# Loading the last expert's first weights earlier and its second weights in four quarters, in a one-core mixture-of-experts layer

## The chip, the cores and the metric

The kernel runs on one core of one Trainium2 chip. The metric is device time in microseconds. TensorE is called PE here, its weight loads PEld, VectorE DVE, ScalarE ACT, GpSimd POOL, and SyncE SP. All weights come from HBM by DMAs that SP issues.

## What is computed

```python
def clamped_swiglu(h):
    gate = jnp.minimum(h[..., :D_EXPERT], SWIGLU_LIMIT)
    up = jnp.clip(h[..., D_EXPERT:], -SWIGLU_LIMIT, SWIGLU_LIMIT)
    return gate * jax.nn.sigmoid(SWIGLU_ALPHA * gate) * (up + 1.0)
...
mix = pool_mixer(h, pool_w[j], pool_scale[j])
h = layer_norm(DEEPNORM_ALPHA * h + mix, ln_g[i, 0], ln_b[i, 0])
ffn = moe(h, router_w[i], router_b[i], w1[i], b1[i], w2[i], b2[i])
h = layer_norm(DEEPNORM_ALPHA * h + ffn, ln_g[i, 1], ln_b[i, 1])
...
# in moe, for the rows of an expert e, top 4 of 32 experts for each token:
h = x_ext[tok] @ w1[e] + b1[e]
return (clamped_swiglu(h) @ w2[e] + b2[e]) * g[:, None]
```

There are 256 tokens after 16 meta tokens, 1024 channels, 32 experts, all in float32. For each expert `w1` is 1024 x 2048 (8 MB) and `w2` is 1024 x 1024 (4 MB). So about 400 MB of weights are read, each once.

## The kernel before

After a prologue (pooling mixer, first layer norm, router, places of the tokens in the experts' slots), a loop in Python goes over the 32 experts. Each expert has 64 slots; two experts make a pair. For expert `e` the loop

- issues the loads of `w1[e]` (four tiles of 2 MB) and then of `w2[e-1]` (two tiles of 2 MB);
- multiplies the gathered tokens `xg` with `w1[e]` (`mlp_in`, line 436);
- finishes the expert before it (`finish(e - 1)`): `mlp_out`, line 486, multiplies the activations `act` with `w2[e-1]` into the bank `ps_y`, and `out_evac`, lines 475 and 477, takes the result to `y` on ACT and DVE, scaled by the gate;
- computes `act` of expert `e` (`swiglu`: copies, transposes on PE in line 448, and elementwise work);
- on even `e`, adds the pair before it to `acc` (`combine`): four matmuls of line 506 with the pair's slot rows `s`, and four adds on DVE in line 508.

All weight tiles come from one pool of 8 buffers (`wpool`), in the order of the load calls. A tile is loaded when the matmuls on the tile eight places ahead of it have ended. All loads stand in SP's one queue, in that order.

After the loop the last expert's `w2` is loaded in two halves of the output columns (`load_w2_halves`, eight DMAs of 512 KB). Four banks `z` take `acc` through an identity matmul (line 615). Then for each half: `mlp_out_half` (line 495), the evacuation to `y`, the slot matmuls of line 621 that add `y` to `z`, and the `bn_stats` of line 108 over 512 columns. At the end `store` does the second layer norm from `z` on DVE and writes the output. A branch for experts with more than 64 tokens follows; it is not taken here.

The engines' order is that of the built program: each engine runs its own list strictly in order. A scheduler places the work of neighbouring calls; it put the identity matmuls of line 615 into the first-weight matmuls of the last expert, and between its transposes.

In the profile each fp32 matmul of the program shows as two rows with a weight load each, so that one weight tile of 2 MB is 16 matmul rows.

Of the kernel before, what the change touches and what calls it, by code (L numbers as in the profile page):

```python
# [9 lines left out]
F32 = mybir.dt.float32  # L10
# [27 lines left out]


@with_exitstack  # L40
def moe_trunk(ctx: ExitStack, tc: tile.TileContext, x, pool_w, aux_in, b1_in, w1, w2, b2, out):
    nc = tc.nc

    const = ctx.enter_context(tc.tile_pool(name="const", bufs=1))
    small = ctx.enter_context(tc.tile_pool(name="small", bufs=2))
    mid = ctx.enter_context(tc.tile_pool(name="mid", bufs=2))
    wpool = ctx.enter_context(tc.tile_pool(name="wpool", bufs=W_BUFS))
# [8 lines left out]
    def bank_t():  # L56
        return bank("t", 2)
# [38 lines left out]
    def spread(row, i, p):  # L96

        for k in range(4):
            spread.last = nc.tensor.matmul(p[:, k * P:(k + 1) * P], rhs=ident, start=True, stop=True,
                                           lhsT=row[:, 4 * i + k:4 * i + k + 1].to_broadcast([P, P]))  # L100
        return p

    def columns():
# [3 lines left out]
    def stats(st, z, i):  # L107
        nc.vector.bn_stats(st[:, i, :], z[i])
# [39 lines left out]
    with tc.tile_pool(name="pro", bufs=1) as pro:  # L148
# [94 lines left out]
        def turn(i):  # L243
            for t in range(NT):
                for k in range(4):
                    nc.tensor.transpose(zs[i][t][:, k * P:(k + 1) * P], zT[:, 4 * i + k, t * P:(t + 1) * P], ident)
                nc.vector.bn_stats(sts[t][:, i, :], zs[i][t])

        turn(1)
# [67 lines left out]
        for k0 in range(0, KC, 2):  # L317
            p = bank_t() if k0 < 4 else bank_o()
            for k in range(2):
                kk = k0 + k  # L320
                for t in range(NT):
                    gl = nc.tensor.matmul(p[:, k * P:(k + 1) * P], lhsT=h[:, t, kk * P:(kk + 1) * P],
                                          rhs=df[:, t, :2 * CAP], start=(t == 0), stop=(t == NT - 1))
# [48 lines left out]
    def load_w2(src):  # L372
        v = src.rearrange("(i p j) f -> i p j f", p=P, j=4)
        ts = []
        for i in range(KC // 4):
            wt = wpool.tile([P, 4, D], F32, tag="w", name="w2t")
            nc.sync.dma_start(out=wt, in_=v[i])
            ts.append(wt)
        return lambda k: ts[k // 4][:, k % 4, :].rearrange("p (c o s) -> p o c s", c=2, o=2)

    def load_w2_halves(src):

        v = src.rearrange("(i p j) f -> i p j f", p=P, j=4)
        ts = []
        for c in range(2):
            wt = wpool.tile([P, KC, 512], F32, tag="w", name="w2h")
            for k in range(0, KC, 2):
                i, j = divmod(k, 4)
                nc.sync.dma_start(out=wt[:, k:k + 2, :], in_=v[i, :, j:j + 2, c * 512:(c + 1) * 512])
            ts.append(wt)  # L390
# [7 lines left out]
    def gather(d):  # L398

        xg = columns()  # L400
        for k0 in range(0, KC, 4):
            p = bank_o() if k0 else bank_m()
            for k in range(4):
                cs = slice((k0 + k) * P, (k0 + k + 1) * P)
                for t in range(NT):
                    nc.tensor.matmul(p[:, k * P:(k + 1) * P], lhsT=h[:, t, cs], rhs=d[:, t, :2 * CAP],  # L406
                                     start=(t == 0), stop=(t == NT - 1))
            nc.scalar.copy(xg[k0 // 4].rearrange("p k s -> p (k s)"), p)  # L408
        return xg
# [31 lines left out]
    def swiglu(ph, bias):  # L441
        pre = []
        for u in range(2):
            hs = work.tile([P, 512], F32, tag="hs", name="hs", bufs=3)
            nc.scalar.copy(hs, ph[u])  # L445
            pt = bank_t()
            for j in range(4):
                nc.tensor.transpose(pt[:, j * P:(j + 1) * P], hs[:, j * P:(j + 1) * P], ident)  # L448
            a = work.tile([P, KC, CAP], F32, tag=f"a{u}", name=f"a{u}", bufs=1)
            nc.vector.tensor_add(a, pt.rearrange("p (c s) -> p c s", s=CAP),  # L450
                                 bias[:, :, u].unsqueeze(2).to_broadcast([P, KC, CAP]))
            pre.append(a)
        gate, up = pre
        nc.vector.tensor_scalar_min(gate, gate, LIMIT)  # L454
        sig = work.tile([P, KC, CAP], F32, tag="sig", name="sig", bufs=1)
        nc.scalar.activation(sig, gate, AF.Sigmoid, scale=SWIGLU_ALPHA)  # L456
        nc.vector.tensor_scalar(up, up, LIMIT, -LIMIT, op0=ALU.min, op1=ALU.max)
        nc.vector.tensor_mul(gate, gate, sig)  # L458
        act = work.tile([P, KC, CAP], F32, tag="act", name="act", bufs=2)
        nc.vector.scalar_tensor_tensor(act.rearrange("p c s -> p (c s)"), up.rearrange("p c s -> p (c s)"), 1.0,  # L460
                                       gate.rearrange("p c s -> p (c s)"), op0=ALU.add, op1=ALU.mult)
        return act


    def rows_of(o, i):

        r = (o ^ i) * CAP
        return slice(r, r + CAP)
# [18 lines left out]
                                 start=(n == 0), stop=(n == KC - 1))  # L487
        out_evac(py, y, slice(0, 512), sg, i)

    def mlp_out_half(act, wt, y, sg, i, c):  # L490
        py = [bank_t()[rows_of(o, i), :256] for o in range(2)]
        for n in range(KC):
            hf, j = divmod(n, 4)
            for o in range(2):
                nc.tensor.matmul(py[o], lhsT=act[:, 2 * j + hf, :], rhs=wt[:, n, o * 256:(o + 1) * 256],  # L495
                                 start=(n == 0), stop=(n == KC - 1))
        out_evac(py, y, slice(c * 256, (c + 1) * 256), sg, i)

    def outputs():
        return work.tile([P, 2, 512], F32, tag="y", name="y", bufs=2)  # L500
# [1 line left out]
    def combine(y, s):  # L502
        for t in range(NT):
            for o in range(2):
                p = bank_o()
                nc.tensor.matmul(p, lhsT=s[:, o, t * P:(t + 1) * P], rhs=y[:, o, :], start=True, stop=True)  # L506
                a = acc[:, t, :].rearrange("p (c o s) -> p o c s", c=2, o=2)[:, o]
                nc.vector.tensor_add(a, a, p.rearrange("p (c s) -> p c s", c=2))  # L508

    def add_bias():  # L510

# [69 lines left out]

    pairs[0] = df, xg0
    first = None
    for e in range(E):
        pair, i = divmod(e, 2)
        w1k = load_w1(w1[e])
        if e:
            w2s[e - 1] = load_w2(w2[e - 1])
        if i == 0:
            xg = pairs[pair][1]  # L590
        ph = mlp_in(lambda k: xg[k // 4][:, k % 4, i * CAP:(i + 1) * CAP], w1k)
        if e == 0:
# [76 lines left out]
```

## Time and profile before

| | |
|---|---|
| time, median of 3 runs | 983.04 us (982.01 to 983.7) |
| time of the profiled execution | 984.9 us |
| span of its instructions | 983.1 us |
| PE busy | 918.0 us, 93% |
| DVE, ACT busy | 228.7 us, 123.0 us |
| DMA, mean over the span | 414 GB/s, 407.13 MB |

The span runs from the first instruction of the program to the end of the last one; the time has what lies around it too, 1.8 us here. A share of busy time is an average over stages with different limits, so the end of the program has to be read by itself, in order of time.

### The profile page before, as it was taken

The numbers are of one execution on the slowest core, as the hardware profiler recorded it, in microseconds if no ns is written. First come the engines' busy times: TensorE is split into PE (matmuls) and PEld (weight loads), VectorE is DVE, ScalarE is ACT, GpSimd is POOL, SyncE is SP. The second block draws the span as 40 slices with busy tenths as digits, with TensorE's granted clock in tenths as the row PEclk, the third lists the DMA queues.
The fourth block names the chain that finished last, engine by engine and source line by source line (L and its number), as shares of the span: only waits on it lengthen the run. The fifth ranks groups of instructions, "written<-read, shape, count | busy, mean of one in ns | idle before, by whom it ended". The sixth has DMA issues, their size and how long they took to land.

```text
span 983.1 us, 10139 instructions
## 1 busy us (share of the span) xinstructions
PE 918.0 (93%) x4401; PEld 372.5 (38%) x4401; DVE 228.7 (23%) x470; ACT 123.0 (13%) x209; POOL 1.1 (0%) x9
## 2 busy tenths in 40 slices
PE   9999999999999999999989999799998989899894
PEld 6445343433334343433424333242433424233233
DVE  7242212112221212212211121211112211121214
ACT  1311111011111111011101111111011101011111
POOL 0000000000000000000000000000000000000000
PEclk9989999999999999999999999999999999999998
DMA  9999999999999999999999999999999999999992
GB/s 363 429 427 428 397 365 424 427 428 427 427 429 428 427 428 428 428 427 427 427 428 426 429 426 427 429 428 427 427 428 428 428 427 426 429 429 428 427 399 80
DMA packets 31072, 407.13 MB, mean 414 GB/s; under 512 B 3344, under 2 KB 3472, under 8 KB 6704
## 3 DMA queue, kind: packets, MB, share of 16 engines
q1 hardware_dynamic: 30976, 406.31, 97.9%
q8 instruction: 36, 0.59, 0.2%
q10 hardware_dynamic: 48, 0.13, 0.0%
q14 instruction: 12, 0.10, 0.0%
HBM read 405.38 MB, written 1.05 MB: 413 GB/s over the span
## 4 chain that ended last, share of the span: by engine, by line
PE 67%; DMA 28%; DVE 2%; ACT 1%; issue 1%; DVEq 0%; ACTq 0%
PE ps_h L436 33%; DMA w2t<-in_w 25%; PE ps_y L486 13%; PE ps_o L506 6%; DMA w1t<-in_w 3%; PE ps_o L406 3%; PE ps_m L406 3%; DVE y L477 1%; PE ps_m L425 1%; PE ps_t L448 1%; PE ps_m L419 1%; PE ps_t L173 1%; PE ps_t L495 1%; ACT hs L445 1%; PE ps_o L521 0%
## 5 line engine op out<-in xcount | busy, mean ns | idle before, releaser
L436 PE MATMUL ps_h<-w1t,xg 128*64 128x512 f32 x2048 | 464.0, 601 | 15.6 <-DMA w1t<-in_w 14.9
L436 PEld LDWEIGHTS ps_h<-w1t,xg 128*64 128x64 f32 x2048 | 141.0, 138 | 300.2 <-issue 260.0
L486 PE MATMUL ps_y<-w2t,act 128*64 128x512 f32 x992 | 222.7, 596 | 10.8 <-DMA w2t<-in_w 10.8
L450 DVE TENSOR_TENSOR a<-ps_t,b 128x512 f32<-128x512 f32 x64 | 44.2, 692 | 386.0 <-PE ps_t L448 382.4
L486 PEld LDWEIGHTS ps_y<-w2t,act 128*64 128x64 f32 x992 | 68.1, 137 | 142.3 <-issue 121.7
L445 ACT COPY hs<-ps_h 128x512 f32<-128x512 f32 x64 | 37.5, 585 | 330.5 <-PE ps_h L436 330.5
L506 PE MATMUL ps_o<-y,srow 128*128 128x512 f32 x120 | 58.4, 618 | 12.9 <-DVE y L477 12.9
L477 DVE TENSOR_SCALAR y<-ps_y,sgate 64x512 f32<-64x512 f32 x31 | 23.2, 750 | 130.5 <-PE ps_y L486 130.5
L508 DVE TENSOR_TENSOR acc<-acc,ps_o 128x512 f32<-128x512 f32 x60 | 41.3, 688 | 28.8 <-PE ps_o L506 28.8
L448 PE MATMUL ps_t<-ident,hs 128*128 128x128 f32 x256 | 42.4, 290 | 4.5 <-ACT hs L445 4.5
L475 ACT ACTIVATE y<-ps_y,sgate 64x512 f32<-64x512 f32 x31 | 21.1, 682 | 194.5 <-DVE y L477 194.5
L448 PEld LDWEIGHTS ps_t<-ident,hs 128*128 128x128 f32 x256 | 27.6, 143 | 38.7 <-ACT hs L445 36.1
L506 PEld LDWEIGHTS ps_o<-y,srow 128*128 128x128 f32 x120 | 19.0, 188 | 53.1 <-DVE y L477 26.1
L427 DVE COPY sgate<-ps_m 128x4 f32<-128x4 f32 x16 | 2.6, 162 | 155.9 <-PE ps_m L425 155.9
L406 PEld LDWEIGHTS ps_o<-disp,h 128*128 128x128 f32 x240 | 29.0, 191 | 22.7 <-issue 22.7
L406 PE MATMUL ps_m<-disp,h 128*128 128x128 f32 x240 | 31.7, 285 | 4.5 <-DVE sgate L427 4.5
L406 PE MATMUL ps_o<-disp,h 128*128 128x128 f32 x240 | 34.4, 287 | 0.0
L406 PEld LDWEIGHTS ps_m<-disp,h 128*128 128x128 f32 x240 | 28.4, 193 | 7.3 <-DVE sgate L427 5.7
L456 ACT ACTIVATE sig<-a 128x512 f32<-128x512 f32 x32 | 20.1, 630 | 68.2 <-DVE a L454 68.2
L458 DVE TENSOR_TENSOR a<-a,sig 128x512 f32<-128x512 f32 x32 | 22.1, 692 | 13.0 <-ACT sig L456 13.0
L408 ACT COPY xg<-ps_o 128x512 f32<-128x512 f32 x15 | 8.8, 585 | 123.1 <-PE ps_o L406 123.1
L460 DVE SCALAR_TENSOR_TENSOR act<-a,a 128x512 f32<-128x512 f32 x32 | 22.1, 691 | 1.1
(151 smaller groups left out, 268.8 us busy)
## 6 DMA issues: line engine op xcount, KB each, us to landing
w1t<-in_w SPq DMA_DIRECT2D x128, 2048.0 KB, 31.3
w2t<-in_w SPq DMA_DIRECT2D x62, 2048.0 KB, 29.4
w2h<-in_w SPq DMA_DIRECT2D x8, 512.0 KB, 22.7
xT<-in_x SPq DMA_DIRECT2D x2, 544.0 KB, 6.0
pw<-in_pool_w SPq DMA_DIRECT2D x2, 512.0 KB, 8.1
out<-xg SPq DMA_DIRECT2D x4, 256.0 KB, 2.9
b<-in_b SPq DMA_DIRECT2D x1, 256.0 KB, 9.1
aux<-in_aux SPq DMA_DIRECT2D x1, 164.0 KB, 3.1
```

Source lines behind the costliest of these rows:

```text
L406: nc.tensor.matmul(p[:, k * P:(k + 1) * P], lhsT=h[:, t, cs], rhs=d[:, t, :2 * CAP], start=(t == 0), stop=(t == NT - 1))
L436: last[0] = nc.tensor.matmul(ph[u][hf * CAP:(hf + 1) * CAP], lhsT=xcols(k), rhs=wk[:, u * D + hf * 512:u * D + (hf + 1) * 512], start=(k = ...
L445: nc.scalar.copy(hs, ph[u])
L448: nc.tensor.transpose(pt[:, j * P:(j + 1) * P], hs[:, j * P:(j + 1) * P], ident)
L450: nc.vector.tensor_add(a, pt.rearrange("p (c s) -> p c s", s=CAP), bias[:, :, u].unsqueeze(2).to_broadcast([P, KC, CAP]))
L458: nc.vector.tensor_mul(gate, gate, sig)
L460: nc.vector.scalar_tensor_tensor(act.rearrange("p c s -> p (c s)"), up.rearrange("p c s -> p (c s)"), 1.0, gate.rearrange("p c s -> p (c s ...
L475: nc.scalar.activation(y[r, o, cols], py[o], AF.Copy, scale=sg[r, o, i:i + 1])
L477: nc.vector.tensor_scalar_mul(y[r, o, cols], py[o], sg[r, o, i:i + 1])
L486: nc.tensor.matmul(py[o], lhsT=act[:, 2 * j + hf, :], rhs=wk[:, o], start=(n == 0), stop=(n == KC - 1))
L506: nc.tensor.matmul(p, lhsT=s[:, o, t * P:(t + 1) * P], rhs=y[:, o, :], start=True, stop=True)
L508: nc.vector.tensor_add(a, a, p.rearrange("p (c s) -> p c s", c=2))
```

## The change

Three things are edited. (1) The loads of `w1[31]` are called right after those of `w1[30]`, ahead of `w2[29]` and `w2[30]`; `mlp_in` and `swiglu` of expert 31 follow at once, and `finish(29)`, the `combine` of pair 14 and `finish(30)` come behind the loop. `act` gets a third buffer. (2) The last expert's `w2` is loaded and used in four quarters of the outputs, from an input of its own (`w2_last`) in which a quarter's 8 KB lie together for each partition; two quarters share one buffer. Each quarter has its own evacuation, slot matmuls and `bn_stats`. (3) The 128-channel blocks of a row stand in the order `PERM` in `acc`, `h`, the gains and the output, so that one quarter gives neighbouring columns in `z`; the host lays out `w2`, `b2` and the output to match.

```diff
+PERM = (0, 2, 1, 3, 4, 6, 5, 7)
...
-        return lambda k: ts[k // 4][:, k % 4, :].rearrange("p (c o s) -> p o c s", c=2, o=2)
+        return lambda k: ts[k // 4][:, k % 4, :].rearrange("p (o f) -> p o f", o=2)
...
+    def load_w2_quarters():
+
         ts = []
+        for q in range(4):
+            if q % 2 == 0:
+                wt = wpool.tile([P, 2, KC, 2, P], F32, tag="w", name="w2q")
+            for k, n in ((0, KC),) if q < 3 else ((0, 4), (4, 2), (6, 2)):
+                nc.sync.dma_start(out=wt[:, q % 2, k:k + n], in_=w2_last[q, :, k:k + n])
+            ts.append(wt[:, q % 2])
         return ts
...
-        act = work.tile([P, KC, CAP], F32, tag="act", name="act", bufs=2)
+        act = work.tile([P, KC, CAP], F32, tag="act", name="act", bufs=3)
...
+    def mlp_out_quarter(act, wq, y, sg, i, q):
+        py = [bank_t()[rows_of(o, i), :P] for o in range(2)]
         for n in range(KC):
             hf, j = divmod(n, 4)
             for o in range(2):
+                nc.tensor.matmul(py[o], lhsT=act[:, 2 * j + hf, :], rhs=wq[:, n, o],
                                  start=(n == 0), stop=(n == KC - 1))
+        out_evac(py, y, slice(q * P, (q + 1) * P), sg, i)
...
+        if e < E - 1:
+            w1s[e] = load_w1(w1[e])
+
+        if e == E - 2:
+            w1s[e + 1] = load_w1(w1[e + 1])
         if e:
             w2s[e - 1] = load_w2(w2[e - 1])
+        w1k = w1s[e]
...
-        else:
+        elif e < E - 2:
             finish(e - 1)
...
-        if e >= 2 and i == 0:
+        if 2 <= e < E - 2 and i == 0:
             s, _, y = pairs[pair - 1]
             combine(y, s)
-    wts = load_w2_halves(w2[E - 1])
+    wts = load_w2_quarters()
+    finish(E - 3)
+    s, _, y = pairs[E // 2 - 2]
+    combine(y, s)
+    finish(E - 2)
...
+    for q in range(4):
+        c, r = divmod(q, 2)
+        mlp_out_quarter(acts[E - 1], wts[q], y, sg, 1, q)
         for t in range(NT):
             for o in range(2):
+                nc.tensor.matmul(z[t][c][:, (2 * r + o) * P:(2 * r + o + 1) * P], lhsT=s[:, o, t * P:(t + 1) * P],
+                                 rhs=y[:, o, q * P:(q + 1) * P], start=False, stop=(o == 1),
+                                 skip_group_check=True)
+            nc.vector.bn_stats(sts[t][:, q, :], z[t][c][:, 2 * r * P:(2 * r + 2) * P])
```

The rows below are the built programs' own order, without times; a number after x counts the program's instructions (two profile rows for each matmul). The line numbers of the changed program are its own.

SP's queue at its end, before: the rows are the loads of `w1[30]`, `w2[29]`, `w1[31]`, `w2[30]` and the halves of `w2[31]`.

```order
L368 DMA w1t<-in_w 128x4096 x4
L377 DMA w2t<-in_w 128x4096 x2
L368 DMA w1t<-in_w 128x4096 x4
L377 DMA w2t<-in_w 128x4096 x2
L389 DMA w2h<-in_w 128x2x512 x8
```

SP's queue at its end, changed: the row x8 is `w1[30]` and `w1[31]`, the row x4 is `w2[29]` and `w2[30]`; a row of `w2[28]` stands ahead.

```order
L380 DMA w2t<-in_w 128x4096 x2
L371 DMA w1t<-in_w 128x4096 x8
L380 DMA w2t<-in_w 128x4096 x4
L391 DMA w2q<-in_w_last 128x2048 x3
L391 DMA w2q<-in_w_last 128x1024
L391 DMA w2q<-in_w_last 128x512 x2
```

The two tiles of `w2[29]` and the four of `w1[31]` changed places; `w2[30]` and `w2[31]` stand where they stood, the latter in six transfers and not eight.

PE from the transposes of expert 30 on, before (`xg_3865` and `xg_3866` are the tokens of pair 15; the first row of line 486 is `w2[29]`, the last `w2[30]`):

```order
L448 MATMUL ps_t<-ident,hs 128x128 x8
L486 MATMUL ps_y<-w2t,act 64x512 x16
L506 MATMUL ps_o<-y,srow 128x512 x4
L436 MATMUL ps_h<-w1t,xg_3865 64x512 x8
L615 MATMUL ps_o<-acc,ident 128x512 x2
L436 MATMUL ps_h<-w1t,xg_3865 64x512 x8
L436 MATMUL ps_h<-w1t,xg_3866 64x512 x16
L448 MATMUL ps_t<-ident,hs 128x128 x4
L615 MATMUL ps_h<-acc,ident 128x512
L448 MATMUL ps_t<-ident,hs 128x128 x4
L615 MATMUL ps_h<-acc,ident 128x512
L486 MATMUL ps_y<-w2t,act 64x512 x16
```

The same stretch of PE, changed (lines 438, 450, 488, 508 and 628 are the old 436, 448, 486, 506 and 615):

```order
L450 MATMUL ps_t<-ident,hs 128x128 x8
L438 MATMUL ps_h<-w1t,xg_3865 64x512 x16
L438 MATMUL ps_h<-w1t,xg_3866 64x512 x16
L450 MATMUL ps_t<-ident,hs 128x128 x8
L488 MATMUL ps_y<-w2t,act 64x512 x16
L508 MATMUL ps_o<-y,srow 128x512 x4
L488 MATMUL ps_y<-w2t,act 64x512 x8
L628 MATMUL ps_h<-acc,ident 128x512 x2
L488 MATMUL ps_y<-w2t,act 64x512 x8
L628 MATMUL ps_o<-acc,ident 128x512 x2
```

The `combine` of pair 14 (506, now 508) moved from ahead of the matmuls on `w1[31]` to behind them, and the four identity matmuls (615, now 628) from among these to the middle and the end of `w2[30]`.

PE behind that, before: the end of `w2[30]`, then the first half of `w2[31]` and the start of the second.

```order
L486 MATMUL ps_y<-w2t,act 64x512 x16
L495 MATMUL ps_t<-w2h,act 64x256 x16
L621 MATMUL ps_h<-y,srow 128x256 x2
L621 MATMUL ps_o<-y,srow 128x256 x2
L495 MATMUL ps_t<-w2h,act 64x256 x16
```

The same place, changed (497 and 636 are the old 495 and 621); the three rows from 497 on come four times in all.

```order
L628 MATMUL ps_o<-acc,ident 128x512 x2
L497 MATMUL ps_t<-w2q,act 64x128 x16
L636 MATMUL ps_h<-y,srow 128x128 x2
L636 MATMUL ps_o<-y,srow 128x128 x2
L497 MATMUL ps_t<-w2q,act 64x128 x16
```

Where two turns of matmuls, evacuation and slot matmuls stood, there are four, each with as many instructions of half the width.

## Rows read from the trace of the kernel before

**Rows 1.** The page: span, and GB/s in 40 equal slices of it.

```profile
span 983.1 us, 10139 instructions
...
GB/s 363 429 427 428 397 365 424 427 428 427 427 429 428 427 428 428 428 427 427 427 428 426 429 426 427 429 428 427 427 428 428 428 427 426 429 429 428 427 399 80
```

**Rows 2.** Busy time by stretch; PEclk is the granted clock's share of full speed.

```profile
core 0: us, PE busy (x) PEld busy (x) DVE busy (x) ACT busy (x) POOL busy (x), PEclk, DMA share, GB/s
900.00:944.00 44.00, 38.18 (x160) 12.19 (x158) 7.69 (x12) 3.16 (x5) 0.00 (x0) 1.00 1.01 428
...
958.00:966.00 8.00, 7.41 (x54) 4.44 (x52) 2.49 (x4) 1.15 (x2) 0.00 (x0) 1.00 0.35 132
966.00:976.00 10.00, 5.01 (x36) 3.16 (x32) 5.77 (x16) 2.89 (x6) 0.00 (x0) 0.90 0.01 3
```

**Rows 3.** The chain that ended last, in order of time: start us, us, what.

```profile
892.47 32.74 DMA w2t<-in_w
...
925.26 3.68 PE ps_y L486 x16
```

**Rows 4.** PE's timeline from 905 to 963: start, us, line, operation, [idle before <-releaser].

```profile
905.68 3.65 PE L436 MATMUL ps_h<-w1t,xg 128*64 128x512 f32 x16 [1.13 <-DMA w1t<-in_w]
...
915.47 3.65 PE L436 MATMUL ps_h<-w1t,xg 128*64 128x512 f32 x16 [1.23 <-DMA w1t<-in_w]
...
920.46 3.65 PE L486 MATMUL ps_y<-w2t,act 128*64 128x512 f32 x16
925.26 3.65 PE L486 MATMUL ps_y<-w2t,act 128*64 128x512 f32 x16 [1.15 <-DMA w2t<-in_w]
929.77 3.89 PE L506 MATMUL ps_o<-y,srow 128*128 128x512 f32 x8 [0.86 <-DVE y L477]
933.59 3.65 PE L436 MATMUL ps_h<-w1t,xg 128*64 128x512 f32 x16
937.18 1.98 PE L615 MATMUL ps_o<-acc,ident 128*128 128x512 f32 x4
939.09 10.52 PE L436 MATMUL ps_h<-w1t,xg 128*64 128x512 f32 x48
...
952.29 7.09 PE L486 MATMUL ps_y<-w2t,act 128*64 128x512 f32 x32
959.20 3.62 PE L495 MATMUL ps_t<-w2h,act 128*64 128x256 f32 x32
```

**Rows 5.** All engines' timeline from 959 to the end of PE's work.

```profile
959.21 3.17 PEld L495 LDWEIGHTS ps_t<-w2h,act 128*64 128x64 f32 x30 [0.28 <-issue]
959.42 0.74 DVE L477 TENSOR_SCALAR y<-ps_y,sgate 64x512 f32<-64x512 f32 x1 [5.53 <-PE ps_y L486]
...
962.87 0.49 DVE L477 TENSOR_SCALAR y<-ps_t,sgate 64x256 f32<-64x256 f32 x1 [2.70 <-PE ps_t L495]
...
963.41 1.13 PE L621 MATMUL ps_h<-y,srow 128*128 128x256 f32 x4 [0.59 <-DVE y L477]
...
965.34 3.67 PE L495 MATMUL ps_t<-w2h,act 128*64 128x256 f32 x32
...
970.56 1.03 PE L621 MATMUL ps_o<-y,srow 128*128 128x256 f32 x4
...
971.62 0.70 DVE L108 BATCH_NORM_STATS2 ln_st<-ps_o 128x6 f32<-128x512 f32 x1
```

**Rows 6.** SP's queue from 914 on: when the last weight loads were issued.

```profile
914.28 5.22 SPq L377 DMA_DIRECT2D w2t<-in_w  x2
924.15 31.14 SPq L389 DMA_DIRECT2D w2h<-in_w  x8
```

**Rows 7.** Groups by line and shape: busy us, mean ns of one, idle before.

```profile
L506 PE MATMUL ps_o<-y,srow 128*128 128x512 f32 x120 | 58.4, 618 | 12.9 <-DVE y L477 12.9
...
L406 PE MATMUL ps_o<-disp,h 128*128 128x128 f32 x240 | 34.4, 287 | 0.0
...
L425 PE MATMUL ps_m<-gates,disp 128*128 128x2 f32 x120 | 14.4, 242 | 0.7 <-ACT srow L421 0.7
```

More of the change, by code (lines that the diff above doesn't have):

```diff
@@ L40, in moe_trunk @@
 @with_exitstack
-def moe_trunk(ctx: ExitStack, tc: tile.TileContext, x, pool_w, aux_in, b1_in, w1, w2, b2, out):
+def moe_trunk(ctx: ExitStack, tc: tile.TileContext, x, pool_w, aux_in, b1_in, w1, w2, w2_last, b2, out):
     nc = tc.nc
@@ L99, in spread @@
             spread.last = nc.tensor.matmul(p[:, k * P:(k + 1) * P], rhs=ident, start=True, stop=True,
-                                           lhsT=row[:, 4 * i + k:4 * i + k + 1].to_broadcast([P, P]))
+                                           lhsT=row[:, PERM[4 * i + k]:PERM[4 * i + k] + 1].to_broadcast([P, P]))
         return p
@@ L245, in turn @@
                 for k in range(4):
-                    nc.tensor.transpose(zs[i][t][:, k * P:(k + 1) * P], zT[:, 4 * i + k, t * P:(t + 1) * P], ident)
+                    nc.tensor.transpose(zs[i][t][:, k * P:(k + 1) * P], zT[:, PERM[4 * i + k], t * P:(t + 1) * P],
+                                        ident)
                 nc.vector.bn_stats(sts[t][:, i, :], zs[i][t])
@@ L321, in moe_trunk @@
                 for t in range(NT):
-                    gl = nc.tensor.matmul(p[:, k * P:(k + 1) * P], lhsT=h[:, t, kk * P:(kk + 1) * P],
+                    gl = nc.tensor.matmul(p[:, k * P:(k + 1) * P], lhsT=h[:, t, PERM[kk] * P:(PERM[kk] + 1) * P],
                                           rhs=df[:, t, :2 * CAP], start=(t == 0), stop=(t == NT - 1))
@@ L378, in load_w2 @@
             ts.append(wt)
-        return lambda k: ts[k // 4][:, k % 4, :].rearrange("p (c o s) -> p o c s", c=2, o=2)
-    def load_w2_halves(src):
-        v = src.rearrange("(i p j) f -> i p j f", p=P, j=4)
+        return lambda k: ts[k // 4][:, k % 4, :].rearrange("p (o f) -> p o f", o=2)
+    def load_w2_quarters():
         ts = []
[L385 to L390, printed above, removed]
+        for q in range(4):
[4 more added lines that the diff above has]
+            ts.append(wt[:, q % 2])
         return ts
@@ L403, in gather @@
             for k in range(4):
-                cs = slice((k0 + k) * P, (k0 + k + 1) * P)
+                cs = slice(PERM[k0 + k] * P, (PERM[k0 + k] + 1) * P)
                 for t in range(NT):
@@ L488, in mlp_out @@
         out_evac(py, y, slice(0, 512), sg, i)
-    def mlp_out_half(act, wt, y, sg, i, c):
-        py = [bank_t()[rows_of(o, i), :256] for o in range(2)]
+    def mlp_out_quarter(act, wq, y, sg, i, q):
+        py = [bank_t()[rows_of(o, i), :P] for o in range(2)]
         for n in range(KC):
@@ L494, in mlp_out_half @@
             for o in range(2):
-                nc.tensor.matmul(py[o], lhsT=act[:, 2 * j + hf, :], rhs=wt[:, n, o * 256:(o + 1) * 256],
+                nc.tensor.matmul(py[o], lhsT=act[:, 2 * j + hf, :], rhs=wq[:, n, o],
                                  start=(n == 0), stop=(n == KC - 1))
-        out_evac(py, y, slice(c * 256, (c + 1) * 256), sg, i)
+        out_evac(py, y, slice(q * P, (q + 1) * P), sg, i)
     def outputs():
@@ L506, in combine @@
                 nc.tensor.matmul(p, lhsT=s[:, o, t * P:(t + 1) * P], rhs=y[:, o, :], start=True, stop=True)
-                a = acc[:, t, :].rearrange("p (c o s) -> p o c s", c=2, o=2)[:, o]
-                nc.vector.tensor_add(a, a, p.rearrange("p (c s) -> p c s", c=2))
+                a = acc[:, t, :].rearrange("p (q o s) -> p o q s", q=4, o=2)[:, o]
+                nc.vector.tensor_add(a, a, p.rearrange("p (q s) -> p q s", q=4))
     def add_bias():
@@ L583, in moe_trunk @@
     first = None
+    w1s = {}
     for e in range(E):
         pair, i = divmod(e, 2)
-        w1k = load_w1(w1[e])
+        if e < E - 1:
+            w1s[e] = load_w1(w1[e])
+        if e == E - 2:
+            w1s[e + 1] = load_w1(w1[e + 1])
         if e:
             w2s[e - 1] = load_w2(w2[e - 1])
+        w1k = w1s[e]
         if i == 0:
@@ L604, in moe_trunk @@
             prepare(pair + 1)
-        if e >= 2 and i == 0:
+        if 2 <= e < E - 2 and i == 0:
             s, _, y = pairs[pair - 1]
             combine(y, s)
-    wts = load_w2_halves(w2[E - 1])
+    wts = load_w2_quarters()
[3 more added lines that the diff above has]
+    finish(E - 2)
     z = [[bank_h() for _ in range(2)], [bank_o() for _ in range(2)]]
-    sts = [small.tile([P, 2, 6], F32, name="ln_st") for _ in range(NT)]
+    sts = [small.tile([P, 4, 6], F32, name="ln_st") for _ in range(NT)]
     for t in range(NT):
         for c in range(2):
-            nc.tensor.matmul(z[t][c], lhsT=ident, rhs=acc[:, t, c * 512:(c + 1) * 512], start=True, stop=False)
+            nc.tensor.matmul(z[t][c], lhsT=ident, rhs=acc[:, t, c * 512:(c + 1) * 512], start=True, stop=False,
+                             skip_group_check=True)
     s, sg, y = pairs[E // 2 - 1]
-    for c in range(2):
-        mlp_out_half(acts[E - 1], wts[c], y, sg, 1, c)
+    for q in range(4):
+        c, r = divmod(q, 2)
+        mlp_out_quarter(acts[E - 1], wts[q], y, sg, 1, q)
         for t in range(NT):
             for o in range(2):
-                nc.tensor.matmul(z[t][c][:, o * 256:(o + 1) * 256], lhsT=s[:, o, t * P:(t + 1) * P],
-                                 rhs=y[:, o, c * 256:(c + 1) * 256], start=False, stop=(o == 1))
-            stats(sts[t], z[t], c)
+                nc.tensor.matmul(z[t][c][:, (2 * r + o) * P:(2 * r + o + 1) * P], lhsT=s[:, o, t * P:(t + 1) * P],
+                                 rhs=y[:, o, q * P:(q + 1) * P], start=False, stop=(o == 1),
+                                 skip_group_check=True)
+            nc.vector.bn_stats(sts[t][:, q, :], z[t][c][:, 2 * r * P:(2 * r + 2) * P])
     store(z, g1_b, b1_b, sts)
@@ L640, with turned @@
     f = {n: np.asarray(a) for n, a in inputs.items()}
+    def turned(a):
+        return a.reshape(-1, KC, P)[:, list(PERM)].reshape(a.shape)
     pw = f["pool_w"].reshape(G, 2, P, GD).transpose(2, 0, 1, 3).reshape(P, -1)
@@ L654 @@
         "w1": f["w1"].reshape(E, KC // 2, 2, P, 2 * D).transpose(0, 1, 3, 2, 4).reshape(E, D, 2 * D),
-        "w2": f["w2"].reshape(E, KC // 4, 4, P, D).transpose(0, 1, 3, 2, 4).reshape(E, D, D),
-        "b2": f["b2"].reshape(E, D),
+        "w2": f["w2"].reshape(E, KC // 4, 4, P, 2, 2, 2, P).transpose(0, 1, 3, 2, 5, 4, 6, 7).reshape(E, D, D),
+        "w2_last": f["w2"].reshape(E, KC, P, 2, 2, 2, P)[-1].transpose(2, 4, 1, 0, 3, 5).reshape(4, P, KC, 2, P),
+        "b2": turned(f["b2"].reshape(E, D)),
     }
@@ L667 @@
     r = run_bass_kernel_spmd(nc, [arrays], core_ids=[0])
-    return r.results[0]["out"].reshape(1, SEQ, D)
+    return turned(r.results[0]["out"]).reshape(1, SEQ, D)
```

## The prediction

> **What bounds the kernel now.** I read the page first. The transfers run at about 428 GB/s in nearly every slice until the last two, and the last slice has 80 [rows 1]. So the body of the program is paced by the weights, and only its end can be moved by an order of loads. The stretches of the end say the same with a border: from 900 to 944 us the DMA share is 1.01 and PE is busy 38.18 of 44.00 us; from 958 on the share falls to 0.35 and then 0.01, while PE is busy 7.41 of 8.00 us [rows 2]. Somewhere between, the pace passes from DMA to PE. The chain of work that ended last names the place: its last DMA piece is the wait for a tile of `w2`, which ends at 925.26 [rows 3]; everything behind it is work of PE, and later of DVE.
>
> PE's timeline shows both regimes. Up to 925.26, a tile is 3.65 us of matmuls, and then PE waits for the next: starts at 905.68, 915.47 and 925.26 are two tiles apart each, so a tile arrives every 4.90 us [rows 4]. Behind 925.26 no row waits for a DMA. PE does the rest of `w2[29]`, the `combine` (929.77), `w1[31]` with the identity matmuls, `w2[30]` (952.29), and at 959.20 begins the last expert's second weights [rows 4]. At 925.26 eight tiles' worth of weights are still to come, 39 us at the cadence, so until about 964.4; PE's work takes 46 us, so the transfers end first, but not by much. Last come two turns of matmuls, evacuation and slot matmuls, up to 970.56 + 1.03 = 971.59, and 11.5 us of layer norm and output up to 983.1 [rows 1, 5].
>
> **The order of the loads.** It adds no bytes. The tiles have equal size and each still waits for the tile eight places ahead, whose release does not move: SP began the loads of `w2[31]` at 924.15 [rows 6], when PE had left the tile of 920.46 [rows 4], and a tile of `w1[31]` in that place is 16 rows of PE too. So I keep the arrivals and rename them. With 925.26 for the second tile of `w1[31]`: third 930.15, fourth 935.05, `w2[29]` 939.95 and 944.84, `w2[30]` 949.74 and 954.63, the quarters each 2.45 us later, 957.08 to 964.42. Now PE's list:
>
> - The fourth tile of `w1[31]` starts at 935.05. As with `w1[30]` (915.47 to 920.46, 4.99 us with the transposes [rows 4]) `w2[29]` starts at 940.04 and has done its first tile at 943.69. It waits until 944.84.
> - From there to the end of `combine` it takes as long as before: 933.59 - 925.26 = 8.33 us [rows 4], so 953.17.
> - `w2[30]` is two halves of (959.20 - 952.29) / 2 = 3.46 us, each followed by two identity matmuls of 939.09 - 937.18 = 1.91 us [rows 4]: 956.63, 958.54, 961.99, 963.90.
>
> The last expert's second weights start at 963.90 where they started at 959.20: **+4.7 us**. The reason in words: before, PE filled the gaps that the weights left with nothing but waits up to 925.26; now it waits up to 944.84, because a tile of `w1[31]` taken at its arrival costs 4.90 us and from the buffers it cost 3.65. The `combine` and the four identity matmuls, which ran while tiles arrived, now run behind nearly the last one. The activation of expert 31 is ready some 20 us earlier, but it never was late: `w2[30]` covered it.
>
> **The quarters.** Before, a turn was 3.62 us of matmuls, 0.59 of evacuation with its waits (0.49 on DVE), and slot matmuls from 963.41 to 965.34, 1.93 us [rows 4, 5]; two turns to the last row's end are 12.39 us. Now there are four turns, each with the same number of rows and half the columns.
>
> - Matmuls: a row of 512 columns costs 7.09 / 32 = 0.222 us, one of 256 columns 3.62 / 32 = 0.113 [rows 4]. It is the columns that count, so 128 columns cost not under 0.057 and, if something else begins to bind, not over 0.113: 1.81 to 3.62 us for 32 rows. I take 1.9, near the straight line, since the weight loads of these rows lie beside the matmuls (3.17 us of loads under 3.62 [rows 5]).
> - Evacuation: 512 columns took 0.74 us on DVE and 256 took 0.49 [rows 5], so 128 take about 0.36, and with the 0.10 around it 0.46. Bounds 0.36 and 0.59.
> - Slot matmuls: eight rows of 128 columns with 128-wide weights. The same form in line 406 costs 34.4 / 240 = 0.143 us [rows 7]: 1.15 us. Bounds 0.97 (half of 1.93) and 1.3.
>
> A turn is 3.51 us, four are 14.04: **+1.65 us** (3.14 by the low bounds: +0.2). PE strictly takes matmuls, then slot matmuls, then the next quarter, so the evacuation is paid four times and hidden by nothing. All data are there: the last piece arrives at 964.42 and the fourth quarter starts at 963.90 + 3 x 3.51 = 974.4, so finer transfers gain nothing. That cover is 10 us; without it each late microsecond would count in full.
>
> **What is left.** The last `bn_stats` reads 256 columns, not 512 (0.70 us [rows 5]), behind PE's last row: 0.35 to 0.70, and with four groups to aggregate, not two, I take **-0.2 us**. The channel order changes views, not counts: adds and matmuls of the 14 earlier pairs lie in stretches where PE waits for weights anyway; if that cover were missing it would show as a longer `combine`. The third `act` buffer, the new input and the longer life of `act` of expert 31 cost no instruction. I take 0 for them.
>
> **Sum.** 4.7 + 1.65 - 0.2 = +6.15 us, made on the profiled execution (span 983.1, time 984.9; it is 1.9 over the median of the runs). On the median 983.04 that is **989.2 us**, 0.6% slower.
>
> **A rule against the quarters.** The trace shows the loads of 64-wide weights beside the matmuls at 256 columns [rows 5]. The Trainium skill, "TensorE: Matmul & The Clock Gate", section "Part 3: Packing small matmuls — row/col tiling", says that a weight load overlaps a running matmul only when the two stand in different row groups; here both take all 128 rows. The same page (section "Part 2: What happens when you issue a matmul") prices a load by its columns, 64 / 1.2 = 53 ns, an estimate by which 32 rows would take 1.7 us more per quarter. The trace does not agree with the strict reading at 256 columns: 32 rows would then have taken 5.3 us, not 3.62.
>
> **Rivals.**
> - *Weight loads bind at 128 columns.* For it: rows of line 425 with 2 columns still cost 14.4 / 120 = 0.12 us with a 128-wide load [rows 7], so a row has a floor. Against it: a 64-wide load is half of that. With 3.62 us a quarter it adds 4 x 1.72 = 6.9 us: 996.1. What the skill's rule gives is this case.
> - *The transfers set the end (faster).* If PE kept up, only a quarter of the last quarter's matmuls (0.5 us), its evacuation and slot matmuls (1.6) and 11.3 us would follow 964.42: 977.8 span, 977.7 us. For it: the DMA share of 1.01 [rows 2]. Against it: PE would have to start the quarters by 952.5, before the second tile of `w2[30]` is there (954.63). To be faster at all it must start them by 957.7, and behind 954.63 stand 3.46 + 1.91 us. It decides only if tiles come some 2.3 us sooner and PE has lost its backlog besides.
> - *Nothing moves.* The load order is in the program, so the change does what it says; a tie needs the low bound of the quarters and arrivals some 2.6 us sooner.
> - *The clock.* It was 1.00 up to 966 and fell only behind PE's last rows [rows 2]; the gaps of a turn get shorter, not longer. At the lower level 4 x 3.05 us would double: 1001.
>
> **Chances and range.** Forecast 0.78, with 987.3 to 991.2 for itself: the low bounds of the turns take off 1.5, their high ones add 1.1, arrivals and the spread of the runs do the rest. Loads bind, wholly or in part, 0.13; clock 0.02; tie 0.03; faster 0.04. The range 987.0 to 993.0 takes in half of the load rival and leaves out under 0.2. A measurement of this kernel tells about 0.2% (2 us) from no change; so faster 0.04, same 0.03, slower 0.93.
>
> **What would show it.** In the changed profile: PE waiting for `w1t` and `w2t` until about 945; the `combine` from 949 to 953; the first row of line 497 near 963.9; its 32 rows in 1.9 us and turns of 3.5 us; no row of 497 waiting for a DMA; PE's end near 977.9. I am wrong in the first term if the quarters start by 960, in the second if the 32 rows take over 2.5 us or under 1.8, and altogether if PE is found waiting for `w2q`.

## The result and the profile after

The changed kernel takes 988.46 us (median of 4 runs, 987.49 to 989.07) against 982.55 for the kernel before (4 runs, 982.01 to 983.7). The ratio is 1.0059, 95% interval 1.0047 to 1.0071: slower by 5.9 us. The forecast was 989.2. All times below leave out one slow run, of 2423.14 us, among the eleven of the kernel that is called quarters_only below.

The page of the changed kernel, with the same two lines as [rows 1]:

```profile
span 985.7 us, 10306 instructions
...
GB/s 380 427 427 429 416 366 425 428 427 427 427 429 428 428 426 428 430 425 429 429 426 427 430 427 428 427 430 425 428 429 428 428 426 429 426 427 430 428 350 46
```

The span is only 2.6 us longer than before's, and that is not the effect. The two profiled executions differ in their bodies, where the edits change the views (the channel order) but no load and no count of instructions: the fourth tile of `w1[30]` starts at 911.19 here and at 915.47 before [rows 4]. Before's profiled execution took longer than all of its timed runs (984.9), after's was the shortest of its four (987.49). So I count every profile from the start of that tile, the last weight tile that stands alike in both programs. From there to the end it is 985.7 - 911.19 = 74.5 us, and before 983.1 - 915.47 = 67.6: 6.9 us more.

The chain that ended last, near its end (start us, us, what), to be held against [rows 3]:

```profile
905.09 35.95 DMA w2t<-in_w
941.09 3.68 PE ps_y L488 x16
```

The last wait for a transfer ended at 925.26, and now at 941.09: measured from the fourth tile of `w1[30]`, at 9.8 us before and at 29.9 now. PE's timeline shows that stretch (columns as in [rows 4]):

```profile
911.19 3.65 PE L438 MATMUL ps_h<-w1t,xg 128*64 128x512 f32 x16 [1.25 <-DMA w1t<-in_w]
...
916.18 3.65 PE L438 MATMUL ps_h<-w1t,xg 128*64 128x512 f32 x16
920.98 3.65 PE L438 MATMUL ps_h<-w1t,xg 128*64 128x512 f32 x16 [1.15 <-DMA w1t<-in_w]
926.40 3.65 PE L438 MATMUL ps_h<-w1t,xg 128*64 128x512 f32 x16 [1.77 <-DMA w1t<-in_w]
931.30 3.65 PE L438 MATMUL ps_h<-w1t,xg 128*64 128x512 f32 x16 [1.24 <-DMA w1t<-in_w]
...
936.28 3.65 PE L488 MATMUL ps_y<-w2t,act 128*64 128x512 f32 x16
941.09 3.65 PE L488 MATMUL ps_y<-w2t,act 128*64 128x512 f32 x16 [1.16 <-DMA w2t<-in_w]
945.61 3.89 PE L508 MATMUL ps_o<-y,srow 128*128 128x512 f32 x8 [0.86 <-DVE y L479]
949.43 3.65 PE L488 MATMUL ps_y<-w2t,act 128*64 128x512 f32 x16
953.01 1.98 PE L628 MATMUL ps_h<-acc,ident 128*128 128x512 f32 x4
954.92 3.65 PE L488 MATMUL ps_y<-w2t,act 128*64 128x512 f32 x16
958.51 1.98 PE L628 MATMUL ps_o<-acc,ident 128*128 128x512 f32 x4
960.42 1.97 PE L497 MATMUL ps_t<-w2q,act 128*64 128x128 f32 x32
962.83 0.71 PE L636 MATMUL ps_h<-y,srow 128*128 128x128 f32 x4 [0.44 <-DVE y L479]
963.38 0.61 PE L636 MATMUL ps_o<-y,srow 128*128 128x128 f32 x4
963.92 1.97 PE L497 MATMUL ps_t<-w2q,act 128*64 128x128 f32 x32
...
973.88 0.61 PE L636 MATMUL ps_o<-y,srow 128*128 128x128 f32 x4
```

The tiles of `w1[31]` are now taken as they arrive, the second to the fourth after 1.15 to 1.77 us of waiting, where before they came 3.5 to 3.6 us apart out of the buffers [rows 4]. The `combine` (945.61) and the identity matmuls (953.01, 958.51) stand behind the last wait. One tile came late: 920.98 to 926.40 is 5.42 us, not 4.90. From 911.19 to the first row of `w2[31]` (960.42) it is 49.2 us; before 43.7. No row of line 497 waits for a DMA.

A turn of a quarter on all engines:

```profile
960.42 1.73 PEld L497 LDWEIGHTS ps_t<-w2q,act 128*64 128x64 f32 x32 [0.76 <-issue]
...
962.42 0.36 DVE L479 TENSOR_SCALAR y<-ps_t,sgate 64x128 f32<-64x128 f32 x1 [3.05 <-PE ps_t L497]
...
963.58 0.43 DVE L639 BATCH_NORM_STATS2 ln_st<-ps_h 128x6 f32<-128x256 f32 x1 [0.80 <-PE ps_h L636]
```

The weight loads, 1.73 us of them, lie beside the 1.97 us of matmuls. A turn is 963.92 - 960.42 = 3.50 us. PE's last row ends at 973.88 + 0.61 = 974.49, 14.07 us after the first row of line 497, and the program 11.2 us later.

The windows of the changed kernel (columns as in [rows 2]):

```profile
900.00:944.00 44.00, 34.75 (x160) 11.25 (x160) 6.87 (x12) 5.18 (x8) 0.00 (x0) 1.00 1.01 428
958.00:966.00 8.00, 7.45 (x80) 5.10 (x76) 2.04 (x5) 1.08 (x3) 0.00 (x0) 1.00 0.09 36
966.00:980.00 14.00, 7.27 (x88) 6.36 (x88) 8.55 (x23) 3.69 (x8) 0.00 (x0) 0.91 0.02 4
```

From 900 to 944 PE is busy 34.75 us, 3.4 less than before, at the same DMA share of 1.01. This window stands 4.3 us further on in the program than before's; over the same stretch of it (895.72 to 939.72) PE is busy 35.52 us, 2.7 less. The granted clock is 1.00, the level of 2.4 GHz, from the first row of line 497 to PE's last; the 0.91 belongs to a window that reaches 5.5 us past PE's last row.

### The profile page after: what moved, and what is told of

It is laid out like the page before. It is cut to its first block, busy times and chain, and to the rows that moved or that the text cites. A ratio compares the mean times of both kernels' runs of the same rounds, so it can differ in the third digit from the quotient of the medians.

```text
span 985.7 us, 10306 instructions
## 1 busy us (share of the span) xinstructions
PE 916.8 (93%) x4481; PEld 375.3 (38%) x4481; DVE 229.7 (23%) x476; ACT 123.8 (13%) x211; POOL 1.1 (0%) x9
## 4 chain that ended last, share of the span: by engine, by line
PE 64%; DMA 32%; DVE 2%; ACT 1%; issue 1%; DVEq 0%; ACTq 0%
PE ps_h L438 31%; DMA w2t<-in_w 28%; PE ps_y L488 13%; PE ps_o L508 6%; DMA w1t<-in_w 4%; PE ps_m L408 3%; PE ps_o L408 3%; PE ps_m L427 1%; DVE y L479 1%; PE ps_t L450 1%; PE ps_m L421 1%; PE ps_t L497 1%; PE ps_t L175 1%; ACT hs L447 1%; PE ps_o L523 0%
```

## The experiments

All ten in one table. The three stretches are from the profiles: A from the start of the fourth tile of `w1[30]` to the first row of `w2[31]`, B from there to the end of PE's last row, C from there to the end. "By profile" is A + B + C less the 67.6 us of before; "by time" is the difference of the medians. The ratio is a figure of its own over the runs, not the quotient of the medians, so that the two can differ by a few tenths of a microsecond. Each kernel shares its chip with runs of the kernel before.

| kernel | A | B | C | by profile | by time | ratio [95%] |
|---|---|---|---|---|---|---|
| before | 43.73 | 12.39 | 11.5 | | | |
| changed | 49.23 | 14.07 | 11.2 | +6.9 | +5.9 | 1.0059 [1.0047, 1.0071] |
| order_only | 48.69 | 12.43 | 11.4 | +4.9 | +4.1 | 1.0037 [1.0023, 1.0051] |
| quarters_only | 43.73 | 14.02 | 11.1 | +1.3 | +0.8 | 1.0009 [1.0000, 1.0018] |
| order_half | 48.06 | 12.39 | 11.4 | +4.2 | +3.9 | 1.0044 [1.0031, 1.0058] |
| coarse | 48.69 | 14.07 | 11.2 | +6.4 | +6.3 | 1.0066 [1.0052, 1.0080] |
| order_half2 | 46.83 | 12.38 | 11.9 | +3.5 | +2.9 | 1.0029 [1.0018, 1.0040] |
| quarters_pipe | 48.69 | 12.01 | 11.1 | +4.2 | +5.3 | 1.0051 [1.0037, 1.0065] |
| no_ident | 42.70 | 12.38 | 12.8 | +0.2 | +0.7 | 1.0008 [0.9999, 1.0017] |
| early_o | 43.16 | 12.38 | 11.9 | -0.2 | -0.2 | 1.0001 [0.9992, 1.0010] |
| pipe_old | 43.73 | 11.99 | 11.1 | -0.8 | -1.1 | 0.9990 [0.9981, 0.9999] |
| no_ident_pipe | 42.70 | 11.70 | 13.3 | +0.1 | +0.2 | 0.9998 [0.9989, 1.0007] |

**order_only.** The kernel before with the new order of loads and of the calls, and with the two halves.

```diff
+        if e == E - 2:
+            w1s[e + 1] = load_w1(w1[e + 1])
         if e:
             w2s[e - 1] = load_w2(w2[e - 1])
...
```

> The kernel before with the load order alone: the last expert's first weights ahead of two experts' second ones, its second weights still in halves. My theory (PE takes these first weights at the pace of arrival, and combine and identity matmuls fall behind the last tiles): the matmuls on the last expert's second weights begin 4.7 us later counted from the last tile of w1[30], and the time is 4.2 to 5.5 us over the kernel before, 0.43 to 0.56%. Rival (the four turns or the new layout carry the loss): within 1 us of the kernel before.

It gives A = 48.69, with no late tile, and 1.0037. That is 4.9 us by profile; by time it is 4.1, a little under the 4.2 to 5.5 expected. Its timeline bears out the first term step by step (below):

```profile
913.24 3.65 PE L436 MATMUL ps_h<-w1t,xg 128*64 128x512 f32 x16 [1.25 <-DMA w1t<-in_w]
...
932.82 3.65 PE L436 MATMUL ps_h<-w1t,xg 128*64 128x512 f32 x16 [1.24 <-DMA w1t<-in_w]
...
937.80 3.65 PE L486 MATMUL ps_y<-w2t,act 128*64 128x512 f32 x16
942.60 3.65 PE L486 MATMUL ps_y<-w2t,act 128*64 128x512 f32 x16 [1.15 <-DMA w2t<-in_w]
947.12 3.89 PE L506 MATMUL ps_o<-y,srow 128*128 128x512 f32 x8 [0.86 <-DVE y L477]
950.94 3.65 PE L486 MATMUL ps_y<-w2t,act 128*64 128x512 f32 x16
...
961.93 3.67 PE L495 MATMUL ps_t<-w2h,act 128*64 128x256 f32 x32
```

**quarters_only.** The changed kernel with the old order of loads and calls, so the opposite part.

```diff
-        if e == E - 2:
-            w1s[e + 1] = load_w1(w1[e + 1])
...
```

> The changed kernel with the old order of loads and of finishing: quarters, new layout and channel order stay. My theory: turns of 3.5 us, four in 14.0 against 12.4, the end of the norm 0.2 to 0.3 us shorter: 1.0 to 1.8 us over the kernel before, 0.10 to 0.18%. Rival (quarters carry the loss): 5 to 6 us over it. Rival (the smaller last piece is worth something in the old order): under the kernel before.

A is that of before to the hundredth, B is 14.02 and C 0.4 less than before:

```profile
913.52 3.65 PE L438 MATMUL ps_h<-w1t,xg 128*64 128x512 f32 x16 [1.25 <-DMA w1t<-in_w]
...
957.25 1.92 PE L497 MATMUL ps_t<-w2q,act 128*64 128x128 f32 x32
...
970.66 0.61 PE L626 MATMUL ps_o<-y,srow 128*128 128x128 f32 x4
```

By time it is +0.8 us or 0.1%, which can hardly be told from nothing, and a little under the 1.0 to 1.8 expected; by profile it is 1.3. The two parts add up in the profiles, 4.9 + 1.3 = 6.2 against 6.4 for the whole without a late tile (coarse). By time 4.1 + 0.8 falls short of 5.9, within the intervals.

**coarse.** The changed kernel, `w2[31]` in two transfers and not six.

```diff
-            for k, n in ((0, KC),) if q < 3 else ((0, 4), (4, 2), (6, 2)):
-                nc.sync.dma_start(out=wt[:, q % 2, k:k + n], in_=w2_last[q, :, k:k + n])
+                nc.sync.dma_start(out=wt, in_=w2_last[q:q + 2].rearrange("q p k o s -> p q k o s"))
```

> The changed kernel with the last expert's second weights in two transfers of 2 MB and not six of 1 MB to 256 KB. My theory (PE is about 10 us behind the transfers when it comes to the last quarter): within 1 us of the changed kernel, so 5 to 7 us over the kernel before, and no matmul of the quarters waits for a transfer. Rival (the fine transfers gain something that other parts give back): 2 us or more over the changed kernel.

The turns stay at 14.07 us, and the time is that of the changed kernel within the intervals. The fineness of the last transfers is worth nothing that can be measured here: no matmul of the quarters waits for them in either kernel.

**order_half.** order_only with two of the four tiles of `w1[31]` ahead of `w2[29]` and two behind, to see whether the loss grows with the move.

```diff
+            w1s[e + 1] = load_w1(w1[e + 1], ts, (0, 1))
         if e:
             w2s[e - 1] = load_w2(w2[e - 1])
+        if e == E - 2:
+            load_w1(w1[e + 1], ts, (2, 3))
...
```

> As the run with the order alone, but only two of the four tiles of w1[31] go ahead of w2[29]; the other two stand behind it. My theory (the loss is what PE can no longer take from the buffers): PE waits for arrivals up to the second tile of w2[29], 9.8 us later than before and 9.8 earlier than with all four, so about half of the loss: 2.0 to 3.2 us over the kernel before. Rival (it is the early activation or the place of the identity matmuls that costs): all of the loss or none of it.

It missed: A grew by 4.33 us, nearly as much as with the whole move. The timeline says why:

```profile
936.55 3.03 PE L506 MATMUL ps_o<-y,srow 128*128 128x512 f32 x6 [0.86 <-DVE y L477]
...
943.10 1.12 PE L506 MATMUL ps_o<-y,srow 128*128 128x512 f32 x2
...
945.01 1.12 PE L628 MATMUL ps_o<-acc,ident 128*128 128x512 f32 x2 [0.78 <-DVE acc L508]
```

The kernel's scheduler had split the `combine` around a tile of `w1[31]`, so that an identity matmul waited 0.78 us for an add on DVE. The run tested another order than the one meant.

**order_half2.** The same loads, with PE's list held as it was before: the whole `combine` ahead of the last two tiles.

```diff
+        if e == E - 1:
+            with tc.issue_after(last[0].ins):
+                finish(E - 3)
+                s, _, y = pairs[E // 2 - 2]
+                combine(y, s)
+            with tc.issue_after(last[0].ins):
+                mlp_in(cols, w1k, ph, range(4, KC))
...
```

> The half move again, with PE's list held as in the kernel before: combine wholly ahead of the last two tiles of w1[31], the identity matmuls behind the first of these. My theory (the loss is what PE can no longer take from the buffers; the first half move lost 1.7 us more to a wait for an add and to alternating rows of two widths): from the last tile of w1[30] to the first row of the last expert's second weights 46.4 us (46.0 to 46.8), where the kernel before has 43.73 and the whole move 48.69; 2.0 to 3.2 us over the kernel before. Rival (the load order costs all at once): 48 us or more there, as in the first half move (48.06).

A is 46.83, 3.1 us more than before and just above the 46.0 to 46.8 expected; the time, 1.0029, is 2.9 us over before and within the 2.0 to 3.2 expected. Behind the last wait (932.17) stand the last two tiles of `w1[31]` again (940.50 and 946.00), at 3.59 us each. The loss does grow with the move, by 3.1 us for half of it and 5.0 for all of it:

```profile
912.42 3.65 PE L436 MATMUL ps_h<-w1t,xg 128*64 128x512 f32 x16 [1.24 <-DMA w1t<-in_w]
...
927.37 3.65 PE L486 MATMUL ps_y<-w2t,act 128*64 128x512 f32 x16 [1.51 <-DMA w2t<-in_w]
932.17 3.65 PE L486 MATMUL ps_y<-w2t,act 128*64 128x512 f32 x16 [1.15 <-DMA w2t<-in_w]
...
940.50 3.65 PE L436 MATMUL ps_h<-w1t,xg 128*64 128x512 f32 x16
...
946.00 3.65 PE L436 MATMUL ps_h<-w1t,xg 128*64 128x512 f32 x16
...
959.25 3.62 PE L495 MATMUL ps_t<-w2h,act 128*64 128x256 f32 x32
```

The tile at 927.37 came 0.3 us late (1.51 of waiting, not 1.2), which is in the 3.1.

**quarters_pipe.** The changed kernel, a quarter's matmuls ahead of the slot matmuls of the quarter before it, in banks of their own for odd quarters.

```diff
-        py = [bank_t()[rows_of(o, i), :P] for o in range(2)]
+        py = [(b() if q % 2 else bank_t())[rows_of(o, i), :P] for o, b in enumerate((bank_y, bank_m))]
...
+    for turn in range(5):
+        if turn < 4:
+            mlp_out_quarter(acts[E - 1], wts[turn], y, sg, 1, turn)
...
```

> The changed kernel with the matmuls of the next quarter ahead of the slot matmuls of each quarter (the results of odd quarters go to two other banks), so that PE does not wait for the evacuation. My theory (the evacuation is paid four times, 0.44 us each): four quarters in 12.2 to 12.7 us and not 14.07, 1.4 to 1.8 us under the changed kernel. Rival (PE would have had to wait for something else there, weights or the next bank): less than 0.5 us.

In the profile the turns shrink from 14.07 to 12.01 us, more than expected: the evacuations then lie beside the next quarter's matmuls. The four waits of 0.44 us make 1.76 us of it; most of the rest is that the next rows now start 1.80 to 1.90 us after a quarter's first row, and its last row ends after 1.97. The times gave back only 0.8 us against the changed kernel (1.0051 and 1.0059), between the theory and the rival, with intervals that overlap.

**no_ident and early_o.** Both take work from PE behind the last wait of before, 3.8 us of identity matmuls. no_ident adds `acc` on DVE at the end instead; early_o takes `acc` of the second token tile into its banks before pair 14 is combined and adds that of the first on DVE.

```diff
 # no_ident
...
                 nc.tensor.matmul(z[t][c][:, o * 256:(o + 1) * 256], lhsT=s[:, o, t * P:(t + 1) * P],
+                                 rhs=y[:, o, c * 256:(c + 1) * 256], start=True, stop=True)
+            nc.vector.tensor_add(zs[t][c], zs[t][c], z[t][c])
...
```

> The kernel before without the four identity matmuls: acc is added to the last expert's result on DVE, half by half. My theory of the end (PE is the bound from 925 us on, and the transfers end some 6.5 us ahead of it): PE loses 3.8 us of work, but meets the last transfers, so its end comes 2.5 to 3.5 us earlier; the adds on DVE take 1.4 us back: 1 to 2.2 us under the kernel before. Rival (the transfers or DVE set the end): within 0.5 us of it, or over it.

> The kernel before with acc of the second token tile taken into its two banks before w1[30], where PE waits for weights anyway; combine of pair 14 adds straight into these banks, and the first token tile's acc is added on DVE at the end. My theory: PE's work behind 925 us is 3.8 us shorter as without identity matmuls, and DVE's end only 0.7 us longer: 1.8 to 3.2 us under the kernel before, which is 0.998 to 0.9967 of it. Rival (the transfers set the end once PE has 3 us less): not more than 1 us under it.

Both missed: level with before. no_ident shows where the 3.8 us went:

```profile
911.95 3.65 PE L436 MATMUL ps_h<-w1t,xg 128*64 128x512 f32 x16 [1.23 <-DMA w1t<-in_w]
...
941.32 3.65 PE L436 MATMUL ps_h<-w1t,xg 128*64 128x512 f32 x16 [0.73 <-DMA w1t<-in_w]
...
951.17 3.65 PE L486 MATMUL ps_y<-w2t,act 128*64 128x512 f32 x16 [1.22 <-DMA w2t<-in_w]
954.65 3.62 PE L495 MATMUL ps_t<-w2h,act 128*64 128x256 f32 x32
```

PE now meets the transfers again, at the fourth tile of `w1[31]` and the second of `w2[30]`, and starts `w2[31]` only 1.0 us earlier (A 42.70). So in the kernel before PE was about 1 us behind the transfers at that tile. DVE took that back and a little more: C is 12.8, not 11.5. In early_o a tile came 0.4 us late besides, and C took back 0.4.

**pipe_old and no_ident_pipe.** Two versions that these runs point to: quarters_only with the pipelined turns of quarters_pipe, and no_ident with both halves' matmuls ahead of the slot matmuls.

```diff
 # pipe_old: quarters_only and quarters_pipe together, slot matmuls held behind the next quarter
+        with tc.issue_after(last[0].ins):
+            for t in range(NT):
...
```

> The old order of loads, quarters, and a quarter's matmuls ahead of the slot matmuls of the quarter before it. In the changed order this pipelining made the four turns 12.0 us in the profile, not 14.07, against 12.39 for the two halves of the kernel before, and the end behind PE is 0.3 shorter. Theory (the turns are the whole cost of the quarters, and only the order of loads costs the rest): 43.7 us from the fourth tile of w1[30] to the first quarter, 12.0 of turns, 0.4 to 0.9 us under before in time, which this measurement can hardly tell from none. Rival (of the 2.1 us that the profile showed in the turns the times kept only 0.8): level with before or 0.5 us over it.

> The kernel before without identity matmuls (acc added on DVE), and the second half's matmuls ahead of the first half's slot matmuls. Without the second edit PE began the halves 1.0 us sooner and the adds on DVE took it back behind PE's end (12.8 us to the end, not 11.5). Theory: the first half's evacuation and half of the adds move beside the second half's matmuls only if the slot matmuls come in time; they come behind them, so the adds of both halves queue on DVE behind PE's end, 0.6 us gained on PE and 1 to 2 us lost on DVE: level with before to 1.5 us over it. Rival (DVE has room there): 1 to 2 us under before.

pipe_old is the only kernel whose interval lies under before: 0.9990 [0.9981, 0.9999], 1.1 us by time and 0.8 by profile. Against the changed kernel that is 0.0069 by the two ratios, 6.8 us; its distance from before is smaller than the 0.2% named ahead. Its turns (line 631 are the slot matmuls; no row of PE here waits for DVE, and the first quarter's evacuation, line 479, lies beside the second quarter's matmuls):

```profile
955.60 1.92 PE L497 MATMUL ps_t<-w2q,act 128*64 128x128 f32 x32
...
957.55 0.36 DVE L479 TENSOR_SCALAR y<-ps_t,sgate 64x128 f32<-64x128 f32 x1 [0.99 <-PE ps_t L497]
...
959.23 0.71 PE L631 MATMUL ps_h<-y,srow 128*128 128x128 f32 x4
...
960.31 1.97 PE L497 MATMUL ps_t<-w2q,act 128*64 128x128 f32 x32
...
966.98 0.61 PE L631 MATMUL ps_o<-y,srow 128*128 128x128 f32 x4
```

no_ident_pipe is level with before, at the low end of what was expected: PE ends its turns 0.7 us sooner, and C grows to 13.3. It is the one kernel in which PE waits for the last transfers:

```profile
913.51 3.65 PE L436 MATMUL ps_h<-w1t,xg 128*64 128x512 f32 x16 [1.25 <-DMA w1t<-in_w]
...
961.87 0.43 PE L495 MATMUL ps_y<-w2h,act 128*64 128x256 f32 x1 [0.22 <-DMA w2h<-in_w]
...
963.17 0.43 PE L495 MATMUL ps_y<-w2h,act 128*64 128x256 f32 x1 [0.21 <-DMA w2h<-in_w]
```

The last piece lets PE go at 963.17, 49.7 us after the fourth tile of `w1[30]`. The prediction's 964.42 is 48.95 after it in its own clock, so this piece came 0.7 us later than counted.

No run pipelines the halves of the kernel before with its identity matmuls in place. Two pipelined halves took 11.70 us in no_ident_pipe, 0.43 of it waiting for transfers, and four pipelined quarters 11.99 in pipe_old. So pipe_old's gain in the turns is that of the pipelining; that quarters are worth anything beyond an end (C) some 0.4 us shorter is not shown.

## Why the prediction was right

**What bounds.** The border between the paces stood where the chain put it. The count of arrivals in steps of 4.90 us held for the tiles to a few hundredths and for the last piece within 0.7 us, as no_ident_pipe shows, but for single late tiles (0.5 us in the changed kernel's profile, 0.3 in order_half2's).

**The order of the loads, forecast +4.7, measured +4.96** (order_only, coarse and quarters_pipe, all 48.69 against 43.73). By steps, in us after the fourth tile of `w1[30]`:

| step | forecast | order_only |
|---|---|---|
| fourth tile of `w1[31]` | 935.05 - 915.47 = 19.58 | 932.82 - 913.24 = 19.58 |
| `w2[29]`, first tile | 24.57 | 24.56 |
| `w2[29]`, second tile | 29.37 | 29.36 |
| end of `combine` | 37.70 | 37.70 |
| `w2[31]` | 48.43 | 48.69 |

Four steps hold to a hundredth. The last is 0.26 short: I took a tile of `w2[30]` at 3.46 us from two tiles that stood back to back, and with identity matmuls behind it one takes 3.58 (949.43 to 953.01 in the changed kernel). That the loss comes from the order alone is shown by order_only and quarters_only, and that it comes from PE taking tiles at their arrival by the waits and by order_half2.

**The quarters, forecast +1.65, measured +1.68.** A turn was to be 3.51 and is 3.50; its parts are 1.97 of matmuls, 0.44 of waiting and 1.09 of slot matmuls, against 1.9, 0.46 and 1.15. That the sum fits to a hundredth is luck in part: the matmuls were taken 0.07 too short, the other two 0.02 and 0.06 too long. That the evacuation is hidden by nothing is shown by quarters_pipe and pipe_old, which hide it and lose 2 us of B. In the times the quarters weigh a little less, +0.8.

**What is left, forecast -0.2.** C is 0.3 shorter in the changed kernel; a `bn_stats` of 256 columns takes 0.43 us, where one of 512 took 0.70 [rows 5].

**The rivals.** Weight loads do not bind: 32 rows took 1.97 us, not 3.62. So the rule of the Trainium skill, "TensorE: Matmul & The Clock Gate", section "Part 3: Packing small matmuls — row/col tiling", does not hold here in its strict reading, by which only a load for another row group runs beside a matmul: the trace has 1.73 us of loads inside 1.97 us of matmuls that take the same 128 rows. The same section also lets a load into a background weight buffer run ahead; no run here shows where these loads go. The transfers do not set the end: no row of line 497 waits for one, and coarse costs nothing that can be measured. The clock was 1.00 over all four turns, and they have one length.

**What I had wrong is how far PE was behind.** "The transfers end first, but not by much" holds for the last piece, which would arrive 5.2 us after `w2[31]` began and 7.2 before PE's end [rows 4, 5]. The margin that counts for a shorter PE list stands at the second tile of `w2[30]`, and it was 1 us, as no_ident shows. The prediction's own numbers held it: by its count that tile arrives at 954.63, and PE reached it at 952.29 + 3.46 = 955.75. The forecast of the change didn't rest on it, since the change lengthens PE's list. The expectations of no_ident and early_o did, and they failed there.

What makes single tiles late stays open. That the pipelined turns are worth 2.1 us in the profile of quarters_pipe and 0.8 in its times can be noise: each of the two ratios is known to some 0.0013, or 1.3 us, to either side. In the old order, with more runs, the same step from quarters_only to pipe_old is 1.9 us by the ratios (1.0009 to 0.9990) and 2.0 by B.

## What to carry to other kernels

Where a DMA-paced loop ends in work that the engine does from full buffers, what counts is the engine's work still ahead when the last wait ends. Here the move put the last wait 19.6 us later, PE did 14.9 us of work ahead of it that it had done behind it, and the kernel lost the difference: 4.7 us by this sum, 5.0 measured. Smaller pieces at the end cost a wait each, unless the next piece's matmuls cover the evacuation; whether they pay where the transfers end last, no run here shows. Before shortening an engine's list, compare each tile's arrival with the time that the engine reaches it, not only the last one.

## What was not expected of the hardware

- A row of 64-wide weights costs nearly by its columns right down to 128: 0.222 us at 512, 0.113 at 256 [rows 4], and 1.97 / 32 = 0.062 at 128.
- A tile of 64-wide weights that is followed by identity matmuls, with 128-wide weights, takes 3.58 us, one followed by its like 3.46: some 0.12 us more. That it is the change of width that costs this is not shown by a run of its own.
- Single tiles arrive 0.3 to 0.5 us late in some executions, and the loop before them can be over 4 us sooner or later (the fourth tile of `w1[30]` at 911.19 and at 915.47), so that the spans of two profiles may not be subtracted: the profiled pair differs by 2.6 us, and the times by 5.9.
